# Two-block network on one core: two modulation pieces a step, reciprocal-root chains first on VectorE, a later mask, last products by column half

## The chip, the cores and the metric

The kernel runs on one core of a Trainium2 chip. The core has five engines with an instruction queue each: TensorE (PE in the profile: matmuls and transposes), VectorE (DVE), ScalarE (ACT), GpSimd (POOL) and SyncE (SP), which here only issues DMAs. 16 DMA engines move data between the chip's memory (HBM) and the on-chip buffer. The metric is the time of one execution on the device, in microseconds (us); lower is better.

## The reference

All is fp32. 256 tokens and 256 context tokens, 1024 wide, go through two blocks. The first has two layers. Each layer is modulated by vectors that come from a product of the conditioning with `w_mod`:

```python
cond, cond_ctx = jax.nn.silu(c), jax.nn.silu(c_ctx)
for i in range(2):
    sh, sc, gt = jnp.split(cond @ w_mod[i] + b_mod[i], 3, axis=-1)
    sh_c, sc_c, gt_c = jnp.split(cond_ctx @ w_mod[i] + b_mod[i], 3, axis=-1)
    h_lat = x * (1.0 + sc[:, None]) + sh[:, None]        # and h_ctx likewise
    ...                                                  # i = 0: latent attention, i = 1: S5
    x = _layernorm(DEEPNORM_ALPHA * x + gt[:, None] * y_lat, ln_g[i], ln_b[i])
```

Layer 0 is attention with a latent of 128 and 16 heads; its input product gives queries, latent, a rotary key and a gate of 2048 columns, and its output product takes `v * silu(gate)`. Layer 1 is an S5 state-space layer in two directions with 128 groups, then a gated linear unit. The second block is a mixer (causal pooling, and spatial gating with a lower-triangular mask on `sgu_w`), cross-attention over 256 memory tokens, a convolutional feed-forward part of width 2816, and a last RMS norm:

```python
xn = rmsnorm(h, norm_mix_g[l]); proj = xn @ w_in[l]
w_masked = jnp.where(jnp.tril(ones((128, 128)))[None], sgu_w, 0)
h = h + jnp.concatenate([y_pool, y_sgu], axis=-1) @ w_out[l]
h = h + mem_cross_attention(rmsnorm(h, norm_xattn_g[l]), mem, ...)
h = h + conv_ffn(rmsnorm(h, norm_ffn_g[l]), w_up[l], conv_w[l], conv_b[l], w_down[l])
return rmsnorm(h, final_norm_g)
```

## The kernel before, in words

Activations stand with features on the 128 partitions and tokens along the free axis. Every fp32 product is made of three matmuls with operands split into a high and a low part (`mm`, L119 to L121: high by high, low by high, high by low). `weight` (L96 to L98) brings 128x1024 of a weight: SyncE loads it (`wr`, three buffers), ScalarE rounds the high part (`wh`), VectorE subtracts for the low one (`wl`).

The order on TensorE is that of the program text (`in_order` with `self.ordered`). On VectorE, ScalarE and SyncE a scheduler sets it when the program is built: among instructions that are ready by its own model it takes the one with the lowest priority number, which counts up with the program; `behind(level)` adds 1000000 per level to it for what is emitted inside, so that such work fills gaps. Work wrapped in it is above all the preparation of the S5 layer, `s5_prep`, in 16 groups of two directions: outer products on VectorE (L37: `sp_t`, `sp_r`, `sp_o`), eight transposes `rtps` (L400) and 32 small products `gps` (L413) on TensorE, and transfers to memory (`d_o` L393, `d_rt` L405).

The stages by time: start to some 56 us; gate projection in `mla_in` to 212 (16 steps `gate(h)`: 24 matmuls `lin`, a SiLU `sg`, its store `d_sg`); the 16 heads, 215 to 505; output product and norm `ln_mod` to 600; S5 to 840; gated unit to 1075; second block to the end.

Modulation products are spread over steps. Only the parts that are needed at once are computed at the start; the others come from the generator `mods()` (`mod`, L577 to L609): 64 pieces of 128x512 (256 KB). A piece is a load `mraw` on SyncE (L589, two buffers) and four matmuls into `modps` (L591), which the trace counts as eight. After a part's last piece ScalarE copies the row (L597, in the ring `sp_rt` of two buffers that the S5 preparation uses too), and TensorE transposes it a step later (L601). `side(n)` (L1598) takes one step of that generator and then some pieces of `s5_prep`. It is called once before `mla_in`, once at the end of each gate step (calls 2 to 17) and three times in each head (calls 18 to 65).

`rms_close` ends a norm: the chain of small VectorE operations `rsqrt` (L153 to L158: start value and three Newton steps), a diagonal `rs_d` (L166), work handed in as `between`, and a product of the diagonal with ones on TensorE (`rsps`, L171) that spreads the root over the partitions. `mean`, `center`, `sums` and `finish` in `ln_mod` do this for two halves of the tokens, r = 0 and 1.

At the end `ffn` accumulates `dn` for two row blocks c and two column halves f over 22 pieces j; `final` adds, squares, takes the root and scales (L1560 to L1575).

Of the kernel before, what the change touches and what calls it, by code (L numbers as in the profile page):

```python
# [11 lines left out]
F32 = mybir.dt.float32  # L12
# [7 lines left out]
ADD, SUB, MUL, MAX, MIN = ALU.add, ALU.subtract, ALU.mult, ALU.max, ALU.min  # L20
# [19 lines left out]
class Net:  # L40
# [33 lines left out]

    @contextmanager
    def behind(self, level=1):

        self.tc.cur_priority += 1000000 * level
        yield
        self.tc.cur_priority -= 1000000 * level  # L80
# [79 lines left out]
    def rms_close(self, r, between=None, tag="ps"):  # L160

        v, tp, n = self.nc.vector, r["tp"], r["n"] // 128
        y = tp.tile([128, 4], F32, name="rs_y")[:, :n]
        self.rsqrt(r["p"][:, 0:n], y, 1.0 / r["feats"], tp)
        d = tp.tile([128, n, 128], F32, name=f"rs_d{n}")
        v.tensor_tensor(d, self.ident.unsqueeze(1).to_broadcast([128, n, 128]),  # L166
                        y.unsqueeze(2).to_broadcast([128, n, 128]), MUL)
        if between:
            between()
        out = self.ps("rsps", tag)[:, :r["n"]]  # L170
        self.in_order(self.nc.tensor.matmul(out, self.ones[1], d.rearrange("p c t -> p (c t)"), start=True, stop=True))  # L171
        return out
# [404 lines left out]
    def mod(self, i, parts, m, tp):  # L577

        nc = self.nc
        for part in parts:
            src = self.I[f"w_mod{i}_{part}"]
            n = src.shape[1]
            p = self.ps("modps")
            for kc in range(8):
                for q in range(n):
                    raw = tp.tile([128, 4, 128], F32, name="mraw", bufs=2)
                    nc.sync.dma_start(raw, src[kc, q])  # L589
                    for j in range(4):  # L590
                        self.in_order(nc.tensor.matmul(  # L591
                            p[32 * j:32 * j + 32, q * 128:q * 128 + 128], self.cs[:, kc, :], raw[:, j],
                            start=(kc == 0 and q == 0), stop=(kc == 7 and q == n - 1), skip_group_check=True))
                    yield
            w = 128 * n
            row = tp.tile([128, 512], F32, name="sp_rt", bufs=2)[:, :w]
            nc.scalar.copy(row, p[:, :w])  # L597
            yield
            p2 = self.ps("modtp")
            for cc in range(n):  # L600
                self.in_order(nc.tensor.transpose(p2[:, cc * 128:cc * 128 + 128], row[:, cc * 128:cc * 128 + 128],  # L601
                                                  self.ident))
            c0 = part * 16
            nc.vector.tensor_tensor(
                m[:, c0:c0 + 4 * n].rearrange("p (j c) r -> p j c r", j=4),
                p2[:, :w].rearrange("p (c j x) -> p j c x", c=n, j=4)[:, :, :, 0:2],
                self.bmod[:, i, c0:c0 + 4 * n].rearrange("p (j c) -> p j c", j=4).unsqueeze(3)
                .to_broadcast([128, 4, n, 2]), ADD)
# [686 lines left out]
    def mixer(self, h, tp, fill, after):  # L1295
        nc, v, I = self.nc, self.nc.vector, self.I
# [5 lines left out]
        sgw = self.load(tp, I["sgu_w"], [128, 4, 128], "sgw")  # L1302
        tri = self.load(tp, I["tri"], [128, 128], "tri")
        sgb = tp.tile([128, 4, 128], F32, name="sgb")
        nc.sync.dma_start(sgb.rearrange("p h t -> p (h t)"), I["sgu_b"].partition_broadcast(128))
        v.tensor_tensor(sgw, sgw, tri.unsqueeze(1).to_broadcast([128, 4, 128]), MUL)
        a, add, close = self.pre(h, g, tp, cut=4)
        fill(1)
        for k in range(8):
# [44 lines left out]
        r = self.rms_open(256, 4, 512, tp, cut=2)  # L1354
# [15 lines left out]
        for c in range(2):  # L1370
            p = self.ps("vtps")
# [13 lines left out]
        for k in range(4):  # L1385
            p = self.ps("zps")
# [10 lines left out]
        for f in range(8):  # L1397
            p = self.linear([I["w_out2"][f]], cat, 256)
# [83 lines left out]
    def ffn(self, h, tp, a, add, close):  # L1482
        nc, v, I = self.nc, self.nc.vector, self.I
        cw = self.load(tp, I["conv_w"], [128, 44, 4], "cw")
        add(7)
        rs = None
        acc = [[self.ps("dn", t) for _ in range(2)] for t in ("bg", "ps")]
        ht = tp.tile([128, 2, 1024], F32, name="ff_h")

        def half(j, w):  # L1490
            return self.linear([I["w_up"][2 * j + w]], a, 256)

        def up(j):
            return [half(j, 0), half(j, 1)]

        def conv(j, ps):
            c = []
            for w, p in enumerate(ps):
                i = 2 * j + w
                x = tp.tile([128, 256], F32, name="ff_p", bufs=2)  # L1500
                v.tensor_tensor(x, p[:, 0:256], rs, MUL)
                t = tp.tile([128, 256], F32, name=f"ff_c{w}", bufs=2)
                nc.scalar.activation(t, x, AF.Identity, bias=cw[:, i, 3:4], scale=cw[:, i, 2:3])
                v.scalar_tensor_tensor(t[:, 1:], x[:, 0:255], cw[:, i, 1:2], t[:, 1:], MUL, ADD)
                v.scalar_tensor_tensor(t[:, 2:], x[:, 0:254], cw[:, i, 0:1], t[:, 2:], MUL, ADD)
                c.append(t)
            nc.scalar.activation(c[0], c[0], AF.Silu)
            v.tensor_tensor(c[0], c[0], c[1], MUL)
            x = tuple(tp.tile([128, 256], F32R, name="ff_x" + y, bufs=3) for y in "HL")
            self.split(*x, c[0])  # L1510
            return x

        def turn(k):

            for c in range(2):
                q = self.ps("htps")
                for i in range(4):
                    self.in_order(nc.tensor.transpose(q[:, i * 128:i * 128 + 128],
                                                      h[:, 4 * k + i, c * 128:c * 128 + 128], self.ident))
                nc.scalar.copy(ht[:, c, 512 * k:512 * k + 512], q)  # L1520

        def down(j, x, w, c):

            t = slice(c * 128, c * 128 + 128)
            for f in range(2):
                fs = slice(f * 512, f * 512 + 512)
                self.mm(acc[c][f], (x[0][:, t], x[1][:, t]), (w[0][:, fs], w[1][:, fs]), j == 0, j == 21)

        p = [half(0, 0)]
        rs = close(lambda: p.append(half(0, 1)))  # L1530
        xs = [conv(0, p)]
        turn(0)
        ws = []
        for j in range(1, 21):
            p = up(j)
            if j == 1:
                turn(1)
            if j == 20:
                last = up(21)
            ws.append(self.weight(I["w_down"][j - 1]))  # L1540
            for c in range(2):
                down(j - 1, xs[j - 1], ws[j - 1], c)
            xs.append(conv(j, p))
        xs.append(conv(21, last))
        ws += [self.weight(I["w_down"][j]) for j in (20, 21)]
        for c in range(2):
            for j in (20, 21):
                down(j, xs[j], ws[j], c)
        return acc, ht

    def final(self, h, acc, g, tp):
# [238 lines left out]
```

## Time and profile before

| | |
|---|---|
| median of 3 runs | 1450.61 us (1449.79 to 1451.89) |
| the profiled execution | 1449.68 us |
| its span | 1447.9 us, mean granted clock 0.965 |
| TensorE / VectorE / ScalarE busy | 1328.2 / 1150.6 / 712.2 us |
| DMA | 291.40 MB, mean 201 GB/s |

The span is the time from the first to the last instruction in the trace. Busy time counts instructions that run, not those that wait. In a timeline row stand the start, the length, the engine, the line in the kernel, the operation, what is written `<-` what is read, a count, and in brackets the idle time before it with the instruction or DMA that ended it. "x8" is eight instructions of one kind in a row. An issue row of SyncE (SPq) is as long as the queue took to issue it; the data land later. PEclk is the share of full TensorE speed that was granted.

### The profile page before, as it was taken

What the parts mean: (1) busy time and instruction counts of PE and PEld (TensorE: products, weight loads), DVE (VectorE), ACT (ScalarE), POOL (GpSimd) and SP (SyncE); (2) the same over time, 40 slices, a digit from 0 to 9 for tenths busy, and PEclk for the clock granted to TensorE, in tenths of its full rate; (3) what the DMA queues carried; (4) which work ended last, traced back from release to release, by engine and by line L of the source; (5) the groups of instructions that cost most, each with busy time, mean ns of one, the idle gap of its engine ahead of it and who ended that gap; (6) DMA issues with size and microseconds to landing.
All of it is one profiled execution on the core that took longest, in us unless ns stands there. A gap on an engine that the chain in (4) does not pass through costs nothing.

```text
span 1447.9 us, 31095 instructions
## 1 busy us (share of the span) xinstructions
PE 1328.2 (92%) x12512; PEld 1196.9 (83%) x12512; DVE 1150.6 (79%) x2123; ACT 712.2 (49%) x1308; POOL 102.9 (7%) x225
## 2 busy tenths in 40 slices
PE   5879979999999988988768699999999999999997
PEld 4656657888888887888757599999998999999996
DVE  7999888998888899389898766555578876888887
ACT  4424436765656536322333264444347556655554
POOL 0012221111001100111111000000000000000000
PEclk9989988999999998999898899999999999999999
DMA  9469996665455544797778665655555453555552
GB/s 347 165 197 282 294 280 168 183 178 157 156 159 158 163 124 154 236 315 256 256 269 298 252 228 181 209 196 193 189 166 180 154 182 103 179 188 188 189 183 96
DMA packets 140625, 291.40 MB, mean 201 GB/s; under 512 B 30480, under 2 KB 70080, under 8 KB 135104
## 3 DMA queue, kind: packets, MB, share of 16 engines
q1 hardware_dynamic: 108592, 232.01, 48.2%
q0 software_dynamic: 11360, 49.34, 10.9%
q10 hardware_dynamic: 20528, 8.06, 2.1%
q8 instruction: 98, 1.61, 0.4%
q14 instruction: 47, 0.39, 0.1%
HBM read 234.83 MB, written 54.53 MB: 200 GB/s over the span
## 4 chain that ended last, share of the span: by engine, by line
PE 67%; DVE 20%; DMA 7%; issue 3%; ACT 3%; SPq 0%; DVEq 0%; ACTq 0%
PE lin L120 14%; PE lin L121 14%; PE lin L119 14%; DVE s_t L493 4%; DVE wl L98 3%; PE vps L472 2%; DVE s_V L495 2%; DMA sp_x<-in_s_bcw_dram 2%; DVE sp_t L37 2%; DMA mraw<-in_w_mod_dram 1%; PE dn L121 1%; PE dn L119 1%; PE dn L120 1%; DMA d_o<-sp_o 1%; DVE s_V L497 1%
## 5 line engine op out<-in xcount | busy, mean ns | idle before, releaser
L97 ACT CAST wh<-wr 128x1024 fp32r<-128x1024 f32 x268 | 280.7, 1049 | 405.4 <-PE lin L120 258.0
L98 DVE TENSOR_TENSOR wl<-wr,wh 128x1024 fp32r<-128x1024 f32 x268 | 327.6, 1223 | 146.3 <-ACT wh L97 145.6
L119 PE MATMUL lin<-prH,wh 128*128 128x256 f32 x512 | 145.3, 284 | 0.0
L119 PE MATMUL lin<-yaH,wh 128*128 128x256 f32 x512 | 144.9, 283 | 0.0
L120 PE MATMUL lin<-yaL,wh 128*128 128x256 f32 x512 | 144.7, 283 | 0.0
L121 PE MATMUL lin<-prH,wl 128*128 128x256 f32 x512 | 143.7, 281 | 1.0 <-DVE wl L98 1.0
L120 PE MATMUL lin<-prL,wh 128*128 128x256 f32 x512 | 144.1, 281 | 0.4 <-DVE prL L109 0.2
L121 PE MATMUL lin<-yaH,wl 128*128 128x256 f32 x512 | 144.2, 282 | 0.0
L120 PEld LDWEIGHTS lin<-prL,wh 128*128 128x128 f32 x512 | 96.6, 189 | 2.1 <-DVE prL L109 1.0
L119 PEld LDWEIGHTS lin<-yaH,wh 128*128 128x128 f32 x512 | 97.6, 191 | 0.0
L121 PEld LDWEIGHTS lin<-yaH,wl 128*128 128x128 f32 x512 | 97.5, 190 | 0.0
L119 PEld LDWEIGHTS lin<-prH,wh 128*128 128x128 f32 x512 | 96.7, 189 | 1.0
L120 PEld LDWEIGHTS lin<-yaL,wh 128*128 128x128 f32 x512 | 97.4, 190 | 0.0
L121 PEld LDWEIGHTS lin<-prH,wl 128*128 128x128 f32 x512 | 96.2, 188 | 1.2 <-DVE wl L98 1.2
L493 DVE TENSOR_TENSOR s_t<-s_V,s_tab 128x256 f32<-128x256 f32 (+2 forms) x120 | 73.1, 652 | 16.0 <-ACT s_V L475 14.7
L121 PE MATMUL u<-h,wl 128*128 128x256 f32 x224 | 64.1, 286 | 9.7 <-DVE wl L98 9.6
L121 PE MATMUL lin<-h,wl 128*128 128x256 f32 x128 | 43.2, 338 | 32.2 <-DVE wl L98 32.2
L427 POOL DMA_DIRECT2D d_t<-sp_g x128 | 67.0, 531 | 59.6 <-DVE sp_g L37 55.4
L119 PE MATMUL u<-h,wh 128*128 128x256 f32 x224 | 64.0, 286 | 0.0
L120 PE MATMUL u<-h,wh 128*128 128x256 f32 x224 | 63.3, 283 | 0.0
L119 PE MATMUL lin<-hH,wh 128*128 128x512 f32 x144 | 60.9, 423 | 0.7 <-ACT hH L103 0.7
L37 DVE TENSOR_TENSOR sp_t<-s_pb,sp_x 128x1024 f32<-128x1024 f32 x64 | 59.9, 953 | 0.6
(505 smaller groups left out, 3837.2 us busy)
## 6 DMA issues: line engine op xcount, KB each, us to landing
wr<-in_glu_dram SPq DMA_DIRECT2D x64, 512.0 KB, 3.3
wr<-in_w_up_dram SPq DMA_DIRECT2D x44, 512.0 KB, 3.3
wr<-in_w_in_dram SPq DMA_DIRECT2D x32, 512.0 KB, 4.8
mraw<-in_w_mod_dram SPq DMA_DIRECT2D x64, 256.0 KB, 3.3
d_rt<-sp_rt SPq DMA_DIRECT2D x64, 256.0 KB, 4.1
d_o<-sp_o SPq DMA_DIRECT2D x32, 512.0 KB, 4.7
wr<-in_s_in_dram SPq DMA_DIRECT2D x32, 512.0 KB, 4.4
s_op<-d_o POOLq DMA_DIRECT2D x16, 1024.0 KB, 7.3
```

The lines of the kernel that those rows point to most:

```text
L37: return lambda *a, **k: self.net.in_order(f(*a, **k))
L97: self.in_order(nc.scalar.copy(hi, raw))
L98: self.in_order(nc.vector.tensor_tensor(lo, raw, hi.bitcast(F32), SUB))
L119: self.in_order(t.matmul(out, a[0], b[0], start=start, stop=False))
L120: self.in_order(t.matmul(out, a[0], b[1], start=False, stop=False))
L121: self.in_order(t.matmul(out, a[1], b[0], start=False, stop=stop))
L427: nc.gpsimd.dma_start(self.d_t[k].rearrange("s i j e c -> i s j e c")[:, :, j, e], a)
L472: self.in_order(nc.tensor.matmul(p[64 * e:64 * e + 64, c:c + 64], rt[:, d, j, r, 64 * e:64 * e + 64], u, start=True, stop=True, skip_group ...
L493: go(v.tensor_tensor(t[:, x], src.to_broadcast([128, 2, 32, n]), a[x].unsqueeze(1).to_broadcast([128, 2, 32, n]), MUL))
L495: go(v.tensor_tensor(dst, dst, t[:, 0], ADD))
L497: go(v.tensor_tensor(dst[:, 1], dst[:, 1], t[:, 1, 0], ADD))
```

## The change

Four edits. In `rms_close` the chain and the diagonal are put under `behind(-1)`, which takes 1000000 off their priority number. In `mod` the generator yields after every second piece. In the mixer the mask's product is put under `behind()`. In `ffn` the last two pieces are multiplied by column half: for each row block first f = 0 of pieces 20 and 21, then f = 1.

```diff
--- before.py
+++ after.py
@@ -75,6 +75,7 @@
     @contextmanager
     def behind(self, level=1):
 
+
         self.tc.cur_priority += 1000000 * level
         yield
         self.tc.cur_priority -= 1000000 * level
@@ -161,10 +162,11 @@
 
         v, tp, n = self.nc.vector, r["tp"], r["n"] // 128
         y = tp.tile([128, 4], F32, name="rs_y")[:, :n]
-        self.rsqrt(r["p"][:, 0:n], y, 1.0 / r["feats"], tp)
-        d = tp.tile([128, n, 128], F32, name=f"rs_d{n}")
-        v.tensor_tensor(d, self.ident.unsqueeze(1).to_broadcast([128, n, 128]),
-                        y.unsqueeze(2).to_broadcast([128, n, 128]), MUL)
+        with self.behind(-1):
+            self.rsqrt(r["p"][:, 0:n], y, 1.0 / r["feats"], tp)
+            d = tp.tile([128, n, 128], F32, name=f"rs_d{n}")
+            v.tensor_tensor(d, self.ident.unsqueeze(1).to_broadcast([128, n, 128]),
+                            y.unsqueeze(2).to_broadcast([128, n, 128]), MUL)
         if between:
             between()
         out = self.ps("rsps", tag)[:, :r["n"]]
@@ -591,7 +593,8 @@
                         self.in_order(nc.tensor.matmul(
                             p[32 * j:32 * j + 32, q * 128:q * 128 + 128], self.cs[:, kc, :], raw[:, j],
                             start=(kc == 0 and q == 0), stop=(kc == 7 and q == n - 1), skip_group_check=True))
-                    yield
+                    if q % 2 == 1:
+                        yield
             w = 128 * n
             row = tp.tile([128, 512], F32, name="sp_rt", bufs=2)[:, :w]
             nc.scalar.copy(row, p[:, :w])
@@ -1303,7 +1306,8 @@
         tri = self.load(tp, I["tri"], [128, 128], "tri")
         sgb = tp.tile([128, 4, 128], F32, name="sgb")
         nc.sync.dma_start(sgb.rearrange("p h t -> p (h t)"), I["sgu_b"].partition_broadcast(128))
-        v.tensor_tensor(sgw, sgw, tri.unsqueeze(1).to_broadcast([128, 4, 128]), MUL)
+        with self.behind():
+            v.tensor_tensor(sgw, sgw, tri.unsqueeze(1).to_broadcast([128, 4, 128]), MUL)
         a, add, close = self.pre(h, g, tp, cut=4)
         fill(1)
         for k in range(8):
@@ -1519,10 +1523,10 @@
                                                       h[:, 4 * k + i, c * 128:c * 128 + 128], self.ident))
                 nc.scalar.copy(ht[:, c, 512 * k:512 * k + 512], q)
 
-        def down(j, x, w, c):
+        def down(j, x, w, c, fs=(0, 1)):
 
             t = slice(c * 128, c * 128 + 128)
-            for f in range(2):
+            for f in fs:
                 fs = slice(f * 512, f * 512 + 512)
                 self.mm(acc[c][f], (x[0][:, t], x[1][:, t]), (w[0][:, fs], w[1][:, fs]), j == 0, j == 21)
 
@@ -1544,8 +1548,9 @@
         xs.append(conv(21, last))
         ws += [self.weight(I["w_down"][j]) for j in (20, 21)]
         for c in range(2):
-            for j in (20, 21):
-                down(j, xs[j], ws[j], c)
+            for f in range(2):
+                for j in (20, 21):
+                    down(j, xs[j], ws[j], c, (f,))
         return acc, ht
 
     def final(self, h, acc, g, tp):
```

The scheduler turns this into other orders. On SyncE in the gate projection (two steps; `mraw` is a modulation piece's load, `d_o` and `d_rt` are stores of the S5 preparation, `d_sg` that of the gate, `wr` a weight load), before:

```order
L589 DMA mraw<-in_w_mod_1_dram 128x512
L739 DMA d_sg<-sg 128x512
L405 DMA d_rt<-sp_rt 128x512 x2
L96 DMA wr<-in_hp_dram 128x1024
L354 DMA sp_x<-in_s_bcw_dram 128x768
L393 DMA d_o<-sp_o 128x8x128
L589 DMA mraw<-in_w_mod_1_dram 128x512
L739 DMA d_sg<-sg 128x512
L405 DMA d_rt<-sp_rt 128x512 x2
L96 DMA wr<-in_hp_dram 128x1024
```

and in the changed kernel:

```order
L591 DMA mraw<-in_w_mod_0_dram 128x512
L742 DMA d_sg<-sg 128x512
L407 DMA d_rt<-sp_rt 128x512 x2
L591 DMA mraw<-in_w_mod_0_dram 128x512
L97 DMA wr<-in_hp_dram 128x1024
L356 DMA sp_x<-in_s_bcw_dram 128x768
L395 DMA d_o<-sp_o 128x8x128
L591 DMA mraw<-in_w_mod_0_dram 128x512
L742 DMA d_sg<-sg 128x512
L407 DMA d_rt<-sp_rt 128x512 x2
L591 DMA mraw<-in_w_mod_0_dram 128x512
L97 DMA wr<-in_hp_dram 128x1024
```

One load of a piece stands behind `d_o` as before; a second stands behind the two `d_rt` and ahead of `wr`.

On TensorE, from the last gate step into the heads, the pieces' rows and their neighbours, before:

```order
L120 MATMUL sctx<-kx0L,qfrH 128x256
L121 MATMUL sctx<-kx0H,qfrL 128x256
L601 MATMUL modtp<-ident,sp_rt 128x128 x2
L591 MATMUL modps<-mraw,cs 32x128 x8
L400 MATMUL rtps<-ident,sp_r 128x128 x8
L413 MATMUL gps<-sp_o,sp_r 32x128 x16
```

and after:

```order
L121 MATMUL sctx<-kx0L,qfrH 128x256
L122 MATMUL sctx<-kx0H,qfrL 128x256
L593 MATMUL modps<-mraw,cs 32x128 x16
L402 MATMUL rtps<-ident,sp_r 128x128 x8
L415 MATMUL gps<-sp_o,sp_r 32x128 x16
L120 MATMUL qabs<-qnH,waH 128x512
```

Two transposes and two pieces have become four pieces in a row. Further on, each later burst has eight matmuls where it had four, and the bursts end in the seventh head (h = 6).

On VectorE in `ln_mod`, from the first chain of the norm (r = 0) to its diagonal, before:

```order
L98 TENSOR_TENSOR wl<-wr,wh 128x1024
L157 TENSOR_TENSOR rs_t<-rs_t,rs_x 128x2
L987 TENSOR_TENSOR total<-total,z 128x256
L158 SCALAR_TENSOR_TENSOR rs_y<-rs_t,rs_y 128x2
L37 SCALAR_TENSOR_TENSOR sp_g<-dmask,dskip,sp_g 128x16
L156 SCALAR_TENSOR_TENSOR rs_t<-rs_y 128x2
L37 SCALAR_TENSOR_TENSOR sp_g<-dmask,dskip,sp_g 128x16
L157 TENSOR_TENSOR rs_t<-rs_t,rs_x 128x2
L37 TENSOR_TENSOR sp_x<-sp_x 128x4x64
L158 SCALAR_TENSOR_TENSOR rs_y<-rs_t,rs_y 128x2
L37 TENSOR_TENSOR sp_t_6520<-s_pb,sp_x 128x1024
L166 TENSOR_TENSOR rs_d_6437<-ident,rs_y 128x256
```

and after:

```order
L157 SCALAR_TENSOR_TENSOR rs_t<-rs_y 128x2
L99 TENSOR_TENSOR wl<-wr,wh 128x1024
L158 TENSOR_TENSOR rs_t<-rs_t,rs_x 128x2
L990 TENSOR_TENSOR total<-total,z 128x256
L159 SCALAR_TENSOR_TENSOR rs_y<-rs_t,rs_y 128x2
L37 SCALAR_TENSOR_TENSOR sp_g<-dmask,dskip,sp_g 128x16
L168 TENSOR_TENSOR rs_d_6437<-ident,rs_y 128x256
L37 SCALAR_TENSOR_TENSOR sp_g<-dmask,dskip,sp_g 128x16
L37 TENSOR_TENSOR sp_x<-sp_x 128x4x64
L99 TENSOR_TENSOR wl<-wr,wh 128x1024
L1009 TENSOR_TENSOR z<-z,rsps 128x256 x3
```

`rs_d` stands ahead of the outer products `sp_t` and of one `wl`; the four `sp_t` and `sp_r` rows come later, between the next half's centring rows (`z` and `sqa`).

## Rows read from the trace of the kernel before

**Rows 1.** Windows of core 0: length, busy by engine, PEclk, DMA share, GB/s

```profile
135.00:155.00 20.00, 18.58 (x185) 13.88 (x186) 19.04 (x27) 7.73 (x16) 6.18 (x15) 1.00 0.99 291
350.00:400.00 50.00, 50.00 (x399) 41.12 (x398) 41.87 (x78) 30.33 (x66) 4.49 (x11) 1.00 0.51 152
```

**Rows 2.** TensorE's timeline, gate projection: start, length, instruction (L591 is a burst)

```profile
142.46 0.42 PE L591 MATMUL modps<-mraw,cs 128*32 128x128 f32 x8
...
150.12 0.42 PE L591 MATMUL modps<-mraw,cs 128*32 128x128 f32 x8
...
158.51 0.43 PE L591 MATMUL modps<-mraw,cs 128*32 128x128 f32 x8
```

**Rows 3.** SyncE's issues in the same steps

```profile
144.13 0.53 SPq L589 DMA_DIRECT2D mraw<-in_w_mod_dram  x1
...
145.95 1.22 SPq L405 DMA_DIRECT2D d_rt<-sp_rt  x2
...
155.82 2.06 SPq L405 DMA_DIRECT2D d_rt<-sp_rt  x2
```

**Rows 4.** Line L589 from 60 to 220 us, its loads' time to landing

```profile
DMA to landing us min/median/max: 2.6/5.0/7.3
```

**Rows 5.** DMA view, 220 to 300 us: count, size, median to landing

```profile
mraw<-in_w_mod_dram SPq DMA_DIRECT2D x16, 256.0 KB, 3.5
```

**Rows 6.** TensorE's timeline in the heads

```profile
226.95 0.65 PE L591 MATMUL modps<-mraw,cs 128*32 128x128 f32 x16
227.53 1.09 PE L400 MATMUL rtps<-ident,sp_r 128*128 128x128 f32 x8
...
243.01 0.43 PE L591 MATMUL modps<-mraw,cs 128*32 128x128 f32 x8
...
244.96 0.43 PE L591 MATMUL modps<-mraw,cs 128*32 128x128 f32 x8
...
253.34 0.43 PE L591 MATMUL modps<-mraw,cs 128*32 128x128 f32 x8
...
256.04 0.43 PE L591 MATMUL modps<-mraw,cs 128*32 128x128 f32 x8
...
332.36 0.43 PE L591 MATMUL modps<-mraw,cs 128*32 128x128 f32 x8
332.72 0.51 PE L119 MATMUL qrope<-qnH,wh 128*128 128x512 f32 x1
```

**Rows 7.** A wait on TensorE, and the window after it

```profile
170.30 1.19 PE L413 MATMUL gps<-sp_o,sp_r 64*32 64x128 f32 x32 [1.57 <-DVE sp_o L37]
...
170.00:172.50 2.50, 2.20 (x35) 1.37 (x36) 2.47 (x4) 0.55 (x1) 1.53 (x4) 0.56 0.82 130
```

**Rows 8.** The end of the gate projection, ScalarE and TensorE

```profile
204.66 0.37 ACT L597 COPY sp_rt<-modps 128x256 f32<-128x256 f32 x1 [2.53 <-DMA d_rt<-sp_rt]
...
215.58 0.79 PE L119 MATMUL qabs<-qnH,waH 128*128 128x512 f32 x1 [4.14 <-ACT waH L103]
```

**Rows 9.** Norm behind the first layer, VectorE and TensorE

```profile
539.40 1.22 DVE L98 TENSOR_TENSOR wl<-wr,wh 128x1024 fp32r<-128x1024 f32 x1
...
542.03 1.23 DVE L37 TENSOR_TENSOR sp_t<-s_pb,sp_x 128x1024 f32<-128x1024 f32 x1
543.17 0.42 DVE L166 TENSOR_TENSOR rs_d<-ident,rs_y 128x256 f32<-128x256 f32 x1
...
543.64 1.22 PE L171 MATMUL rsps<-rs_d,ones 128*128 128x256 f32 x2 [3.96 <-DVE rs_d L166]
...
543.60:546.20 2.60, 2.56 (x10) 2.38 (x11) 2.60 (x6) 0.44 (x1) 2.25 (x5) 0.50 0.97 340
...
575.11 0.39 PE L121 MATMUL lin<-h,wl 128*128 128x256 f32 x1 [2.48 <-DVE wl L98]
```

**Rows 10.** Second block's mixer: TensorE at the norm, VectorE at the mask

```profile
1103.93 0.70 PE L171 MATMUL rsps<-rs_d,ones 128*128 128x256 f32 x2 [1.46 <-DVE rs_d L166]
...
1092.14 0.69 DVE L1306 TENSOR_TENSOR sgw<-sgw,tri 128x512 f32<-128x512 f32 x1 [0.54 <-DMA tri<-in_tri_dram]
```

## The prediction, on record before the run

> **What bounds the kernel now.** I read the windows first, since the share of a whole span hides that the stages have different limits. In the gate projection (some 60 to 212 us) nothing is idle for long: between 135 and 155 us TensorE is busy 18.58 of 20 us, VectorE 19.04 and the DMA engines stand at a share of 0.99. In the heads (215 to 505 us) TensorE alone is full, 50.00 of 50 us with a DMA share of 0.51 [rows 1]. So in the first stage every added byte is suspect, and in the second every added wait of TensorE, and every instruction taken off it, counts in full.
>
> Next come the modulation pieces themselves. A burst is the matmuls of one piece, eight rows in the trace. In the gate projection bursts stand at 142.46, 150.12 and 158.51, so two steps take 16.05 us, 8.03 us each [rows 2]. SyncE issues the load for the next burst at 144.13, and behind it the step's other transfers: the two d_rt end 4.71 us after their burst in one step (145.95 + 1.22 - 142.46) and 7.76 us in the next (155.82 + 2.06 - 150.12) [rows 3]. A piece needs 5.0 us from issue to landing at the median of this stage, 2.6 at the least [rows 4], and 3.5 in the heads [rows 5].
>
> Third, the waits of TensorE in the stretches that the other edits touch: the boundary between gates and heads [rows 8], the norm behind the first layer [rows 9], the second block's mixer [rows 10].
>
> **Two pieces a step, in the gate projection.** Pieces and their bytes are the same in all, 64, but 32 of them now fall on the first 17 calls where 16 did. For TensorE a second piece in a burst costs 0.22: the double burst lasts from 226.95 to 227.53, 0.58 us, a single one 332.36 to 332.72, 0.36 [rows 6]. Fifteen steps of it are 3.3 us. For the DMA engines it is 15 x 0.262 MB = 3.9 MB, which at the 291 GB/s of a window with nothing free [rows 1] takes 13.5 us.
>
> There is a new loop as well. Before, two buffers held two bursts, so a load had almost two steps. Now both belong to one burst: a load can go out only when that burst is done and must be there for the next. The order puts the second of the two behind the same step's d_rt, which wait for transposes that stand behind the burst. So second loads go out 4.7 us after a burst in the short steps; with the median landing they arrive at 9.7, where the step is 8.03: 1.7 x 15 = 25 us. With the landing of the heads they arrive at 8.2, 0.2 x 15 = 3 us. With the late d_rt of the other step kind (7.76) all would be worse, but there the d_rt are late for VectorE's sake, and a TensorE that waits gives VectorE time. While TensorE waits for a piece, the transposes rtps, the products gps and the next 24 projection products stand behind it, and d_rt and d_o behind those. The weight load wr now stands behind the second piece on SyncE, which costs it only that issue, half a microsecond. Ends: +3 (TensorE's matmuls alone) and +25; the byte count at the observed rate lies between and is the nearest row, and a step that stretches also relieves the queues. I take +12.
>
> **Two pieces a step, in the heads.** Before, 48 bursts of 0.36 us = 17.3; after, 16 bursts of 0.58 = 9.3. That is -8.0 at full TensorE. Against it stand waits. A load follows the burst that frees its buffer (0.36) and needs 3.5 [rows 5], so a piece is there 3.9 us after the burst before. Where two calls stand side by side (226.95), pieces three and four wait 3.9 - 0.6 = 3.3. Of the other bursts three follow the one before by 1.95 us (as 243.01 to 244.96) and wait 1.9 each, one by 2.70 (253.34 to 256.04) and waits 1.2 [rows 6]. The sum is 3.3 + 5.8 + 1.2 = 10.3. Then the clock: after a wait of 1.57 us the granted clock was 0.56 over 2.5 us [rows 7], which is near the lower level, 1.2 GHz, and gave away 1.1 us. I let three of the five waits be followed by that, +3. Together -8.0 + 10.3 + 3 = +5. Ends: -8 (all loads in time) and +12 (every wait with a dip, and loads held behind d_o on SyncE, 4 us).
>
> The Trainium skill (DMA: Bandwidth & Descriptors, "Anatomy of one DMA") fits a transfer as about 2.0 us fixed plus its bytes over 436 GB/s. That fit is for the GpSimd path. For 262 KB it gives an estimate of 2.6 us. The trace has this as the shortest load of the stage, 2.6, and almost double at the median [rows 4], so the measurement decides here. By the page the heads' waits would be about 6 and the gates' loop would be hidden; that is the quick rival below.
>
> **The row copy that leaves the boundary.** At 204.66 ScalarE copied the finished row after 2.53 us for a d_rt buffer, in front of the last gate's work. TensorE then waited 4.14 us at 215.58 [rows 8]. In the changed kernel that row is copied at call 9. The gate's d_sg then leaves earlier by about the 2.53; I take -2.5, between 0 (the queue is the limit there) and -4.
>
> **Precedence of the reciprocal roots.** It only reorders VectorE. In the norm behind the first layer rs_d ends the wait of 3.96 us on TensorE. One wl of 1.22 us and one sp_t of 1.23 us before it move behind it [rows 9]: about -2.4 on TensorE. The clock was 0.50 in the 2.6 us after this wait [rows 9]; a shorter one may keep some of the 1.3 us that this cost. In the second half wl moves ahead of the eight scaled tiles, and the wait of 2.48 us at 575.11 [rows 9] goes. Late next are these scaled tiles, by 1.2 us, and the centring of the second half, behind which the moved sp_t pieces now stand, so I credit 1.5. With a microsecond of clock the stage gives -5; ends -8.5 (both waits and their clock) and 0 (the moved pieces hold the second half's sums as long). In the mixer rs_d ends a wait of 1.46 us [rows 10], of which one product of 0.4 us goes; with the mask, which waited 0.54 us for its DMA in front of others [rows 10], -0.5 in all, ends 0 and -1. Other uses of the helper stand in an order that barely changes: 0.
>
> **Last products by column half.** The first half of the last rows is complete three products earlier, but the second is added after the same last matmul as before, and squares and the root wait for that one: 0, ends 0 and -0.3.
>
> **Sum.** +12 + 5 - 2.5 - 5 - 0.5 = +9.0 us on the profiled execution's 1449.68, 1458.7. The median of the runs shown is 0.9 above that execution, so the forecast is 1459.6, said as 1459.
>
> **Rivals.**
> Quick loads, faster: landing falls to 2.6 to 3.5 us. In the gates the second piece arrives at 4.7 + 3.3 = 8.0, inside the step, and only TensorE's +3.3 stays. In the heads waits are 2.4 + 3 x 1.05 + 0.3 = 5.8, so -2.2. Boundary -4, norm -8.5, mixer -1. Sum -12: 1438. For it: the norm's and boundary's waits are plain, and VectorE's 19.04 of 20 leaves open that the DMA share merely follows it. Against it: 5.0 at the median. It decides from landings under 3.4 us in the gate stage.
> Gains and losses cancel: gates +6 (half of the bytes find room, since the share is less at the stage's start), heads 0, the others -8: 1449.
> The loop holds every step: gates +25, heads +8, the others -6: 1477. For it: SyncE's order puts a wait for a later transpose ahead of the load in every step. Against it: a stretched step also moves fewer bytes per microsecond, so landings shorten.
>
> **Chances.** Forecast 0.44, quick loads 0.30, cancelling 0.16, full loop 0.10. The range 1439 to 1476 takes in the ends of the quick case and nearly all of the loop; the forecast's own range is 1453 to 1468. About 0.2%, 2.9 us, is what a measurement here can tell from no change. Faster takes the quick case and a sliver of the cancelling one, 0.33; same 0.12; slower 0.55.
>
> **What would show it.** Right: gate steps of about 8.8 to 9.5 us between bursts, with waits of TensorE for mraw in a gate step; in the heads five waits for mraw of 1 to 4 us, none after some 310 us; rs_d near 2.4 us earlier against its norm's last product, and no wait of 2.48 us for wl. Wrong: bursts still 8.0 us apart with no wait for mraw in the gates, which is the quick rival; or a heads stage shorter by 8 us. If the norm's waits stay as long as they were, the precedence term has failed and the time lies 5 us higher.

## The result and the profile after

The changed kernel takes 1461.09 us at the median (1454.7 to 1466.27, 6 runs), the kernel before 1450.19 (1445.9 to 1451.89, 6 runs). The ratio is 1.0082, 95% interval 1.0054 to 1.0109. The profiled execution took 1460.83 us with a span of 1459.1. Single executions of one kernel lie up to some 9 us from its median, so a few microseconds in one trace prove little by themselves; below, medians decide and traces show the place.

Where the time goes is read by matching TensorE's instructions. Its order is fixed, so the start of the same product after, less its start before, is the delay gathered so far. First at transposes rtps, then the first product qabs of head 0, then the last transposes of the heads, and so on:

| place (time before, us) | delay after, us |
|---|---|
| rtps at 99.8, gate projection | +3.3 |
| rtps at 150.5 | +19.8 |
| rtps at 203.1, its end | +19.6 |
| qabs at 215.6, head 0 | +14.9 |
| qabs at 302.0, of head 6, computed in the turn of head 5 | +30.7 |
| rtps at 501.5, end of the heads | +15.8 |
| rtps at 582.2, norm's second half | +13.1 |
| vps at 611.4, start of S5 | +15.8 |
| rsps at 895.8 and to the end | +11.3 to +11.0 |

The gate projection loses 16.3 us, and all of it before 150 us: from there to its end, with two pieces a step as before that place, the delay stays. The boundary gives 4.7 back. The first six turns of the heads (h = 0 to 5) lose 15.8 and the later ones return 14.9. The last burst stands in the turn h = 5, not in h = 6 as said with the change. The norm gains 2.7 and gives it back. In S5, whose work the change barely touches, 4.5 us come back; the traces of the experiments below give back 0 to 4.2 there, 3.1 in e1 and e3 and 4.2 in e2, whatever edits they have. So most of it belongs to the one execution of before, and the rest is scatter.

The windows of the gate projection in the kernel after (length, busy by engine, PEclk, DMA share, GB/s):

```profile
100.00:150.00 50.00, 40.13 (x340) 29.89 (x338) 35.74 (x49) 15.72 (x31) 9.83 (x22) 0.90 0.81 254
150.00:215.00 65.00, 57.55 (x556) 42.84 (x557) 56.22 (x77) 22.96 (x44) 13.29 (x31) 0.97 0.95 297
```

and the same of before:

```profile
100.00:150.00 50.00, 46.42 (x424) 34.66 (x422) 44.97 (x63) 18.50 (x38) 10.17 (x25) 1.00 0.95 287
150.00:215.00 65.00, 55.62 (x491) 41.16 (x490) 53.96 (x74) 24.23 (x48) 16.42 (x37) 0.92 0.94 281
```

Up to 150 us every engine does less than before, TensorE 40.13 us of work against 46.42, and the DMA engines too, 0.81 against 0.95. A stage in which bytes were the bound would show the opposite. Over the same work (from rtps to rtps, 99.8 to 150.5 us before, 103.1 to 170.3 after) TensorE's idle time grows from 3.6 to 13.1 us, and the granted clock falls from 1.00 to 0.90 over 67 us, which gives away 6.7: together 16.2 of the 16.5 us lost there. Something circular holds the stage. TensorE's waits from 95 to 205 us name it, after (waiting instruction, releaser, us in total, times, longest):

```profile
PE gps L415 <- DVE sp_o L37: 10.6, 4, 3.9
PE modps L593 <- DMA mraw<-in_w_mod_dram: 4.4, 7, 0.9
```

and before:

```profile
PE gps L413 <- DVE sp_o L37: 5.0, 5, 1.6
```

The waits for mraw that were forecast are there, seven of at most 0.9 us. The larger ones are the products gps, which wait for sp_o from VectorE. One of them in the trace after, on TensorE:

```profile
122.73 0.42 PE L593 MATMUL modps<-mraw,cs 128*32 128x128 f32 x8
124.03 0.43 PE L593 MATMUL modps<-mraw,cs 128*32 128x128 f32 x8 [0.87 <-DMA mraw<-in_w_mod_dram]
...
129.38 1.19 PE L415 MATMUL gps<-sp_o,sp_r 64*32 64x128 f32 x32 [3.91 <-DVE sp_o L37]
```

on VectorE:

```profile
128.55 0.69 DVE L37 TENSOR_TENSOR sp_o<-sp_t 128x512 f32<-128x512 f32 x1 [3.63 <-DMA d_o<-sp_o]
129.16 0.69 DVE L37 TENSOR_TENSOR sp_o<-sp_t,sp_t 128x512 f32<-128x512 f32 x1
```

on SyncE:

```profile
119.06 0.41 SPq L591 DMA_DIRECT2D mraw<-in_w_mod_dram  x1
...
120.19 0.42 SPq L395 DMA_DIRECT2D d_o<-sp_o  x1
123.22 1.88 SPq L591 DMA_DIRECT2D mraw<-in_w_mod_dram  x2
```

and the granted clock behind it:

```profile
128.00:140.00 12.00, 10.62 (x80) 7.84 (x80) 7.96 (x11) 1.90 (x4) 0.11 (x1) 0.72 0.51 172
```

sp_o has one buffer. VectorE stood 3.63 us for the store d_o of the sp_o before it, which was issued at 120.19 and let VectorE go at 128.55. gps then waited 3.91 us, and in the 12 us from 128 the granted clock was 0.72. The loop is write sp_o, issue d_o, land, write again. In a step of 8.03 us [rows 2] it had hardly any slack: a write took 1.3 us (128.55 to 129.85), and d_o took 6.5 us to land at the median from 100 to 150 us before, and 7.2 in the same stretch after (the DMA views):

```profile
d_o<-sp_o SPq DMA_DIRECT2D x6, 512.0 KB, 6.5
```

```profile
d_o<-sp_o SPq DMA_DIRECT2D x4, 512.0 KB, 7.2
```

VectorE's waits for d_o between 95 and 160 us rise from 2.2 us to 10.3, the first row of before, the second of after:

```profile
DVE sp_o L37 <- DMA d_o<-sp_o: 2.2, 2, 1.8
```

```profile
DVE sp_o L37 <- DMA d_o<-sp_o: 10.3, 5, 3.6
```

A slower landing is the smaller half of it. Two stores also went out late. SyncE issues in the order of its queue, so a load that waits for its buffer holds what stands behind it. In the second case the two loads at 139.01 had waited for the burst at 138.53, and d_o stood behind them, with its sp_o written by 138.04:

```profile
137.36 0.68 DVE L37 TENSOR_TENSOR sp_o<-sp_t,sp_t 128x512 f32<-128x512 f32 x1
...
139.01 0.81 SPq L591 DMA_DIRECT2D mraw<-in_w_mod_dram  x2
139.97 0.33 SPq L742 DMA_DIRECT2D d_sg<-sg  x1
...
142.21 1.10 SPq L97 DMA_DIRECT2D wr<-in_w_in_dram  x1
143.37 0.48 SPq L395 DMA_DIRECT2D d_o<-sp_o  x1
```

and a store of before, which went out at once:

```profile
135.68 0.68 DVE L37 TENSOR_TENSOR sp_o<-sp_t,sp_t 128x512 f32<-128x512 f32 x1
...
136.39 0.38 SPq L393 DMA_DIRECT2D d_o<-sp_o  x1
```

The two stores went out 4.9 and 5.3 us after their sp_o was written; before, none between 100 and 150 us took over 0.1. The delay jumps behind each of the two: from +7.0 to +13.1 us between the transposes rtps at 117.4 and 126.0, and from +13.7 to +18.0 between those at 133.7 and 142.8. SyncE's own waits for bursts, which free the buffers of mraw, from 95 to 155 us, before and after:

```profile
SPq L589 <- PE modps L591: 6.4, 1, 6.4
```

```profile
SPq L591 <- PE modps L593: 17.7, 4, 8.9
```

In the heads TensorE's bursts after show the forecast waits for the second load (rows that answer to [rows 6]):

```profile
242.66 0.65 PE L593 MATMUL modps<-mraw,cs 128*32 128x128 f32 x16
245.85 0.43 PE L593 MATMUL modps<-mraw,cs 128*32 128x128 f32 x8 [2.54 <-DMA mraw<-in_w_mod_dram]
...
261.96 0.65 PE L593 MATMUL modps<-mraw,cs 128*32 128x128 f32 x16
...
265.20 0.43 PE L593 MATMUL modps<-mraw,cs 128*32 128x128 f32 x8 [1.02 <-DMA mraw<-in_w_mod_dram]
...
315.79 0.43 PE L593 MATMUL modps<-mraw,cs 128*32 128x128 f32 x8 [2.47 <-DMA mraw<-in_w_mod_dram]
...
330.48 0.64 PE L593 MATMUL modps<-mraw,cs 128*32 128x128 f32 x16
```

2.54 us stand where two calls are side by side, 1.02 and 2.47 at two of the short gaps; the last burst is at 330.48, where before bursts went on to 501.15. From the first qabs to that of head 6, the windows before and after and the waits for mraw after:

```profile
215.60:302.00 86.40, 84.07 (x771) 68.55 (x771) 78.23 (x150) 60.46 (x140) 8.82 (x20) 0.95 0.62 174
```

```profile
230.50:332.70 102.20, 91.14 (x893) 75.04 (x893) 80.23 (x154) 62.47 (x142) 8.79 (x20) 0.92 0.61 187
```

```profile
PE modps L593 <- DMA mraw<-in_w_mod_dram: 8.7, 10, 2.5
```

Idle time grows by 8.7 us, which are the waits, and the clock gives away 8.2 us where it gave away 4.3: 12.6 in all. The price of a burst stands in the same stage before:

```profile
395.92 0.28 PE L121 MATMUL pv<-ptcH,ctL 128*128 128x256 f32 x1
396.13 0.43 PE L591 MATMUL modps<-mraw,cs 128*32 128x128 f32 x8
396.48 0.50 PE L119 MATMUL qabs<-qnH,waH 128*128 128x512 f32 x1
```

Products pv follow one another by 0.12 us; here qabs comes 0.56 behind the last of them, so the burst took 0.44.

The norm behind the first layer, TensorE after (rows that answer to [rows 9]):

```profile
557.16 0.70 PE L173 MATMUL rsps<-rs_d,ones 128*128 128x256 f32 x2 [1.79 <-DVE rs_d L168]
...
582.21 0.70 PE L173 MATMUL rsps<-rs_d,ones 128*128 128x256 f32 x2 [0.91 <-DVE rs_d L168]
...
595.28 0.30 PE L402 MATMUL rtps<-ident,sp_r 128*128 128x128 f32 x1 [2.14 <-DVE sp_r L37]
```

The wait for rs_d fell from 3.96 to 1.79 us and the one of 2.48 for wl is gone [rows 9]. New is a wait of 2.14 for sp_r: the outer products that made way come late for the next transposes.

### The profile page after: what moved, and what is told of

Same layout as the page of the kernel before. It is cut to its first block, busy times and chain, and to the rows that moved or that the text cites. A ratio compares the mean times of both kernels' runs of the same rounds, so it can differ in the third digit from the quotient of the medians.

```text
span 1459.1 us, 31089 instructions
## 1 busy us (share of the span) xinstructions
PE 1329.1 (91%) x12512; PEld 1207.8 (83%) x12512; DVE 1149.4 (79%) x2123; ACT 710.3 (49%) x1308; POOL 102.5 (7%) x225
## 4 chain that ended last, share of the span: by engine, by line
PE 64%; DVE 15%; DMA 9%; issue 7%; ACT 3%; SPq 1%; POOL 0%; ACTq 0%; DVEq 0%; POOLq 0%
PE lin L120 14%; PE lin L121 14%; PE lin L122 14%; DMA mraw<-in_w_mod_dram 4%; DVE s_t L495 3%; DVE wl L99 2%; DMA d_o<-sp_o 2%; PE dn L122 1%; PE dn L120 1%; PE dn L121 1%; DVE s_V L497 1%; DVE sp_t L37 1%; PE vps L474 1%; PE slat L120 1%; PE slat L122 1%
## 5 line engine op out<-in xcount | busy, mean ns | idle before, releaser
L495 DVE TENSOR_TENSOR s_t<-s_V,s_tab 128x256 f32<-128x256 f32 (+2 forms) x120 | 73.1, 652 | 13.9 <-ACT s_V L477 12.6
L120 PE MATMUL u<-h,wh 128*128 128x256 f32 x224 | 66.1, 295 | 0.0
L121 PE MATMUL u<-h,wh 128*128 128x256 f32 x224 | 65.6, 293 | 0.0
```

The source lines that it names most:

```text
L120: self.in_order(t.matmul(out, a[0], b[0], start=start, stop=False))
L121: self.in_order(t.matmul(out, a[0], b[1], start=False, stop=False))
L495: go(v.tensor_tensor(t[:, x], src.to_broadcast([128, 2, 32, n]), a[x].unsqueeze(1).to_broadcast([128, 2, 32, n]), MUL))
```

## The experiments

Theory S (store loop): the added loads make d_o land later, and the single sp_o buffer turns that into waits. Theory L (load loop, the forecast's): the second piece arrives late. Theory B3: the bytes bind by themselves. All but e2 contain the other three edits. Each ratio is against runs of the kernel before on the same chip; those of the first four share one median, 1450.46.

**e1: the other three edits alone.**

```diff
-                    if q % 2 == 1:
-                        yield
+                    yield
```

> The changed kernel with one piece a step as before; precedence, late mask and column halves stay. If pairs of pieces are the whole loss (theory A: about +13 us to the end of the gate projection, some 0 in the heads), this is 2 to 4 us below the kernel before, 1446 to 1449, with rs_d's wait at the first norm near 1.8 us. If the norm's reordering costs something of its own (rival B: the moved sp_t pieces come back as a wait of 2 us for sp_r some 30 us later), it is within 1 us of the kernel before.

1450.33 us, ratio 1.0001 (0.9984 to 1.0018). It lies where rival B put it: precedence, late mask and column halves together are worth nothing that can be told. A gain of 2 us, the least of theory A, stays inside the interval. By delays, the trace of e1 gains 2.4 us from the last heads to 582.2 and is back at the start of S5 (+4.9, +2.5, +4.8).

**e2: pairs of pieces alone.** The kernel before with the edit in `mod` only.

> The kernel before with two pieces a step and nothing else. Theory A: 12 to 14 us above the kernel before, 1462 to 1465. Rival B: about 10 above, as in the changed kernel.

1459.79 us, ratio 1.0064 (1.0043 to 1.0085). The loss is the pairs'. Its size is nearer to the 10 of rival B than to the 12 to 14 of theory A, though the interval, 6 to 12 us, does not part them.

**e3: a second sp_o buffer in the gate projection.** `self.extra` is the pool of `mla_in` during its first 13 gate steps, else nothing.

```diff
+                self.extra = tp if h < 13 else None          # in gate(h)
...
-                O = tp.tile([128, 2, 4, 9, 16], F32, name="sp_o")
+                O = self.extra.tile([128, 2, 4, 9, 16], F32, name="sp_o2") if self.extra and d else tp.tile([128, 2, 4, 9, 16], F32, name="sp_o")
```

> The changed kernel with a second sp_o buffer for direction 1 in the gate projection, so that a new sp_o need not wait for the store d_o of the one before to land. Store loop (theory S: the added loads delay d_o's landing, and gps waits for sp_o): the gate stage loses its waits of 2 to 4 us for sp_o and shortens by 8 to 13 us, total 1449 to 1453. Load loop (theory L: the second piece of a burst arrives late): total unchanged within 2 us, 1459 to 1463.

1451.13 us, ratio 1.0002 (0.9985 to 1.0019): as fast as before. The waits of TensorE from 95 to 205 us in e3:

```profile
PE modps L593 <- DMA mraw<-in_w_mod_dram: 9.8, 5, 3.0
PE gps L415 <- DVE sp_o L37: 2.7, 1, 2.7
```

and VectorE's waits for d_o from 95 to 215 us:

```profile
DVE sp_o L37 <- DMA d_o<-sp_o: 0.8, 1, 0.8
```

VectorE's wait for d_o went all but 0.8 us, and with it all but 2.7 us of the wait for sp_o. With the second buffer the scheduler also orders SyncE's queue in another way between 100 and 150 us: no d_o goes out over 2.2 us after its sp_o, and SyncE's waits for bursts from 95 to 155 us are 6.1 us, not 17.7. So the buffer and the order changed together. The load loop is the next in line: waits for mraw grew to 9.8 us. The delay at qabs of head 0 is +4.1 where the changed kernel had +14.9.

**e4: four buffers for pieces in the gate projection.**

```diff
-                    raw = tp.tile([128, 4, 128], F32, name="mraw", bufs=2)
+                    raw = (self.extra.tile([128, 4, 128], F32, name="mraw4", bufs=4) if self.extra
+                           else tp.tile([128, 4, 128], F32, name="mraw", bufs=2))
```

> The changed kernel with four buffers for pieces in the gate projection, two in the heads as before, so that a piece has almost two steps to arrive. Load loop (theory L): waits for mraw vanish in the gates and the stage shortens by 8 to 13 us, total 1449 to 1453. Store loop (theory S): only the gates' own waits for mraw go, some 5 us in all, and waits for sp_o stay at 2 to 4 us each; total 1456 to 1460. If bytes alone bound (theory B3), nothing changes.

1460.78 us, ratio 1.0065 (1.004 to 1.0091): no better than the changed kernel. TensorE's waits from 95 to 205 us:

```profile
PE gps L415 <- DVE sp_o L37: 14.8, 4, 7.0
```

No wait for mraw is left in that stretch, and the waits for sp_o grew to 14.8 us. TensorE's waits for the second piece (theory L) fall as the cause of the loss, and the time is a little above what theory S expected. SyncE's queue kept its order and still waited 16.2 us for bursts from 95 to 155 us.

**e5: half of the added loads left out.** In the first 13 gate steps the second piece of a pair is not loaded; its matmuls use the first one's data.

```diff
-                    raw = tp.tile([128, 4, 128], F32, name="mraw", bufs=2)
-                    nc.sync.dma_start(raw, src[kc, q])
+                    if q % 2 == 0 or not self.extra:
+                        raw = tp.tile([128, 4, 128], F32, name="mraw", bufs=2)
+                        nc.sync.dma_start(raw, src[kc, q])
```

> The changed kernel, but in the first 13 gate steps the second piece of a pair is not loaded: its matmuls read the first one's data again, so half of the modulation weights of those steps are left out. Bytes behind the store (theory S): with as many load bytes per step as before, d_o lands in time, the waits of 2.5 to 4 us for sp_o go, and the total is 1449 to 1453. If the doubled burst on TensorE or the order on SyncE were the cause (rival O), the gate stage stays 10 or more us long and the total 1458 to 1462.

1450.01 us, ratio 0.9989 (0.9972 to 1.0005), with the median of before at 1451.66 in this set. Doubled bursts without doubled loads cost nothing that can be told; it is the loads, in the queue with d_o, that delay the store. Bytes alone (B3) are excluded too, since e3 moves all of them and is as fast as the kernel before. Its trace is of an execution 5 us above the median. There VectorE's waits for d_o from 95 to 205 us are small:

```profile
DVE sp_o L37 <- DMA d_o<-sp_o: 2.7, 6, 0.7
```

TensorE still waits 7.5 us for sp_o, five times and 3.0 at most, so that these waits go was not met in this execution.

Whether bytes, number or place of the loads matters was not parted. The order on SyncE, half of rival O, is not excluded: leaving out loads changes it too. In every trace that loses in the gates (the changed kernel, e2, e4, e9) two stores between 100 and 150 us go out 2.7 to 6.5 us after their sp_o, and SyncE waits 16.2 to 18.0 us for bursts from 95 to 155 us; in those of before, e1, e3, e5, e7, e8 and e10 no store is over 2.2 us late and it waits 5.6 to 6.5.

**e6: one piece a step to the end of the gate projection, two in the heads.**

```diff
-                    if q % 2 == 1:
+                    if q % 2 == 1 or self.single:            # self.single = h < 15, in gate(h)
```

> The changed kernel with one piece a step up to the end of the gate projection and two from the first head on. By the trace of the changed kernel the heads lose some 16 us to waits and their clock before 302 us and get back some 15 as later bursts vanish; here 48 pieces in 24 bursts: 48 x 0.44 - 24 x 0.66 = 5 us saved, against six to eight waits for mraw of 1 to 2.5 us with their clock, 10 to 16 us. Expected 1453 to 1461; if waits in the heads were free, 1445.

1461.59 us, ratio 1.0081 (1.0052 to 1.011), just above what was expected. Pairs in the heads alone cost as much as the whole change when 24 bursts stand there. TensorE's waits from 215 to 480 us:

```profile
PE modps L593 <- DMA mraw<-in_w_mod_dram: 11.8, 13, 2.6
```

and the clock (windows 215 to 300 of e6 and of before):

```profile
215.00:300.00 85.00, 73.55 (x719) 58.96 (x722) 64.44 (x124) 51.89 (x117) 8.77 (x20) 0.90 0.63 190
```

```profile
215.00:300.00 85.00, 82.09 (x723) 67.13 (x723) 76.83 (x150) 59.90 (x139) 8.82 (x20) 0.94 0.62 176
```

The 13 waits sum to 11.8 us, and the granted clock is 0.90 against 0.94.

**e7: one piece a step with the second sp_o.** e1 with the edit of e3.

> One piece a step, the other three edits, and the second sp_o buffer in the gate projection. If the store loop holds the kernel before too, its 7.6 us of waits for sp_o in the gates mostly go: 1443 to 1447. If DVE or the DMA share bound those steps anyway, no change: 1449 to 1452.

1450.56 us, ratio 0.9989 (0.997 to 1.0007): no gain that can be told. Without the added loads the buffer is of no use: waits for sp_o are still there (10.4 us from 56 to 215), not for d_o but for VectorE's own queue.

**e8: pairs in the gate projection alone, with both buffers.** e3 and e4 together, and one piece a step from the first head on.

```diff
-                    if q % 2 == 1:
+                    if q % 2 == 1 or not self.paired:        # self.paired = h < 15, in gate(h)
```

> Two pieces a step in the gate projection alone, with the second sp_o buffer and four mraw buffers there, one piece a step in the heads (where two buffers give two steps of lead), and the other three edits. If the heads' loss is the short lead alone, the heads have 32 single bursts where the kernel before had 48, 16 x 0.44 = 7 us less with no wait for mraw, and the gates cost up to 5 us: 1444 to 1449. If the gates stay bound by bytes, 1453 or more.

1446.09 us, ratio 0.9971 (0.9955 to 0.9986): faster than the kernel before by 4 us, with an interval that excludes no change, and so faster than the changed kernel. The heads have no wait for mraw, and their delay falls from +2.9 at qabs 302.0 to -0.1 at 474.4 as the bursts end.

**e9: e8 without either buffer.**

> Two pieces a step in the gate projection, one in the heads, the other three edits, no added buffer: e8 without its second sp_o and its four piece buffers. If the store loop costs the gates what it did in the changed kernel and the heads lose only their waits, +10 to +14 in the gates and -7 in the heads: 1453 to 1458. If the store loop needed the heads' pairs, 1444 to 1449 as in e8.

1456.26 us, ratio 1.0046 (1.0027 to 1.0065), with before at 1448.79 in this set. As forecast for the store loop. Its trace, of an execution of 1449.22 us, 7 below the median of e9, still shows four waits for sp_o of 11.1 us in the gates (56 to 215 us).

**e10: e8 without the four piece buffers.**

> e8 without its four piece buffers: two pieces a step in the gate projection with the second sp_o, one in the heads. If the store loop is all that pairs cost in the gates, as fast as e8, 1444 to 1449; if the piece buffers carried part of it, 1449 to 1453.

1447.74 us, ratio 0.9988 (0.9969 to 1.0007). The time lies in the range of the first answer, but the kernel before was at 1448.79 here too, 2.9 below its median beside e8; by ratio e10 lies between e8 and e9. The second sp_o, with the order that comes with it, carries the larger part of e9's loss, 1.0046 to 0.9988, and whether the piece buffers add the rest is open, since the intervals of e8 and e10 overlap.

## Why the prediction came out as it did

The time, 1461 against 1459, and the side were right. The steps were not all so, and that the sum came out is in part luck: against the trace the gates were put 4.3 us too low and the norm's gain 5 too high, the boundary's gain 2.2 too low and the heads' loss 4.1 too high, which largely cancel. The stated range, 37 us wide, also took in one of the three rivals and nearly reached the other two.

Gates, +12 forecast, +16.3 in the trace. The place was right, and that a transfer issued behind others would close a loop. The loop named was the wrong one. The step "second loads go out 4.7 us after a burst ... where the step is 8.03" took up the loads' lead only; it did not put the same question to d_o, whose buffer is single and whose landing of 6.5 us plus the writing filled the step already. It did say that d_o stands behind a TensorE that waits; what held d_o was SyncE's queue, where loads waited for bursts ahead of it. e4 took TensorE's waits for loads away and gained nothing that can be told, e3 took the store's loop away and gained all, though with another order on SyncE. Nor did the loop hold all of the 15 steps over which the prediction multiplied: the delay jumps at two places (in e2, e4 and e9 at the same two, by 4.0 to 8.1 us each) and from 150.5 to 203.1 it does not grow, in those three by 3 us at most. In the last four gate steps SyncE's queue has the same pattern in the changed kernel and in e3, with one sp_o buffer and with two, and there neither loses: from rtps at 166.8 to 203.1 the delay goes from +21.0 to +19.6 and from +8.1 to +8.4. How much of the loss is the single buffer's and how much that of the order on SyncE stays open. The clock, 6.7 us of the loss in that stretch, was no term of the gates' sum. The price of bytes at 291 GB/s, on which the +12 rested, was right by accident: the DMA share fell to 0.81 up to 150 us, and e3 carries the same bytes with a delay of only 4.1 us at head 0.

Order on SyncE. That the second load stands behind d_rt was read rightly, but it was one half of it: in part of the steps both loads went out together before d_sg (as at 123.22 in the trace), and what counted was what shared the queue with d_o.

Heads, +5 forecast, +0.9 in the trace. The mechanism was right in both halves, and one term was too small: the savings. 31 single bursts fell away after some 303 us and returned 14.9 us (14.7 to 14.9 in the traces of e2 to e5 too), 0.48 each, with the transposes of a finished row among them. A burst alone is 0.44; 0.36 [rows 6] was the distance from the burst to the next product and left out that the burst itself starts later than a product would. The waits with their clock were right: up to qabs 302.0 stand 16 double bursts where 17 single ones stood, about 3 us more work, so of the 15.8 us lost there 12.6 are waits and clock, where 10.3 and 3 were forecast. The sum of the waits, 8.7, came from ten shorter ones and not from five. With two buffers pairs wait in the heads and single pieces do not, as e6 and e8 show: with pairs the delay grows from +1.4 at head 0 to +13.7 at 474.4, with single pieces it falls from +2.7 to -0.1. Pairs with more buffers there were not run.

Boundary, -2.5 forecast, -4.7 in the trace. The traces with pairs in the gates have -2.7 (e2) to -6.5 (e8) at the same place and those with one piece (e1, e6, e7) +0.3 to +0.9, so the gain is there and its size is known only to a few microseconds.

Norm, -5 forecast, about -3 at 582.2 and nothing at the start of S5. The waits shrank as forecast, 2.2 us and 2.48; "late next" named the scaled tiles and the centring but not the transposes rtps, which need the moved outer products. By e1's interval the three edits gain 2.3 us at most. Single traces can't say more: of the two without the norm's edit, e2's takes 2.8 us longer over this stretch than before's. Mixer: the mask's wait is gone and the delay falls by 0.3, of the -0.5 forecast. Last products: nothing, as forecast.

Of the rivals, the quick loads failed on their condition: loads did not land sooner. From 60 to 225 us in the trace after, line L591:

```profile
DMA to landing us min/median/max: 2.6/4.8/6.9
```

The median is 4.8 us where 3.4 was the point from which that rival decides. The full loop was not reached: TensorE's waits for mraw in the gates were 4.4 us in all, where that rival took 25. Cancelling did not happen, though e3 shows how near it was: with one more sp_o buffer the change comes out even.

## What to carry to other kernels

When transfers are added to a stage, list every buffer there that is written, sent off and written again, and compare its write plus its landing time with the step. Then look at what stands ahead of its store in the issue queue, above all loads that wait for a buffer. Here the single-buffered one with the least slack broke first, though the added transfer was another. Doubling the work per step halves the lead that a fixed number of buffers gives, so here it cost where calls stand close together. A chain that is moved ahead on a full engine moves something else back: follow that work to its next reader before crediting the gain.

## What the runs showed of the hardware

A wait need not be long to cost the clock. After 1.57 us the granted clock was 0.56 for 2.5 us [rows 7]; after the 3.91 us in the trace above it was 0.72 over 12 us. Nor does every longer wait cost it: behind the 2.54 us at 245.85 in the heads it was 1.00 up to 299 us. A 512 KB store took 6.5 to 7.2 us from issue to landing at the median in the gate projection, whether the DMA share was 0.95 or 0.81 over the stretch: a low mean share says little about the landing of one store that goes out in a crowd.
